# Sixteen batched products summed into one weight gradient: a new hand-written order, with A packed in three banks, set-aside places and GpSimd additions

## The chip, the cores and the metric

The kernel runs on one core of a Trainium2 chip. A core has a matrix engine (TensorE, "PE" in the profile, with its weight loads listed apart as "PEld"), a vector engine (DVE), a scalar engine (ACT), GpSimd (POOL) and a queue engine (SP). They work in parallel, each through its own instructions in order, and wait for one another through semaphores. PE writes its results into PSUM, eight banks of 512 fp32 columns on 128 partitions; everything else lies in SBUF. Transfers to and from the chip's memory are DMAs, issued here by SP, ACT and POOL. The metric is the device time of one execution in microseconds, lower is better, as the median of several runs.

## The reference

```python
batch, m, k, n = 16, 512, 1024, 768
input: (batch, m, k) float32;  grad_output: (batch, m, n) float32

def reference(input, grad_output):
    return np.einsum('bmk,bmn->kn', input, grad_output)   # (1024, 768) float32
```

Seen as one product, it is X.T @ G with X of 8192 x 1024 and G of 8192 x 768. The sum runs over all 8192 rows.

## The kernel before

The 8192 rows are cut into 32 "pairs" of 256 rows. Row 2p and row 2p+1 of a pair lie on the same partition, so a pair is two slices of 128 rows. Inputs are turned into bf16 by the loading DMAs (lines 152 and 153, on POOL's queue); the very first slice is loaded as fp32 through SP and ACT and rounded on DVE and ACT (`round_by`).

The output of 1024 x 768 is cut into four quarters by halves of k and n: A (first half of k, left half of n), B (first, right), C (second, left), D (second, right). Each quarter has four blocks q = 0 to 3 of 128 x 384.

A pair is multiplied in one of two ways, by its letter in `LOADS` (line 12):

- "s", plain: each of its two slices adds one matmul to each of the 16 blocks, 32 matmuls of 384 columns;
- "P", Strassen (in Winograd's form): the pair is treated as a 2 x 2 block product, with its two slices as the inner halves. Seven products per q replace eight: A, B, C and four more called 1, 5, 6 and 7, so 28 matmuls. For that DVE forms sums of operands: `sum_x` (tokens x0 to x2; lines 183, 185, 187) and `sum_g` (g0 to g2; lines 193, 195, 197). Results go into tiles `xe` and `ge`, and partly back into the pair itself.

In the end the products are combined: 6 gets 1 added, 7 gets 6 added, 5 gives two differences, and each of the quarters gets one of the shared sums added (`SHARED`, line 253).

There are 32 blocks (8 kinds times 4 q) that grow over the whole run, and eight PSUM banks. So a block is accumulated in a bank for some matmuls, then closed, that is, brought to its fp32 place in SBUF (`acc` for A to D, `macc` for 1, 5, 6, 7), and taken up again later. There are two ways round:

- *fill, then close by copy*: ACT copies the block's partial sum from SBUF into a bank (`fill`, line 274), PE goes on adding to it, and ACT (token c, line 327) or DVE (token v, line 329) copies the bank back;
- *start fresh, then close by addition*: PE starts a bank from nothing, and DVE adds the bank to the SBUF place (token v, line 331).

The final closing of a block (lines 307 to 312) adds the shared sum on DVE, and for A to D stores the block at once with a DMA (line 320).

The order of all this is written out by hand in `PLAN` (lines 22 to 77) as tokens, carried out one after the other; each engine's instructions come in the order of the tokens. `A0@7.1` opens block A0 in bank 7 and does one matmul; `A1.2` does two more matmuls on an open block; `fC0@2` fills bank 2 with C0; `vC0` and `cC0` close on DVE and on ACT; `x0.6` forms the first x-sums of pair 6; `r0` is a rounding. The last fill, `fB3@2+7`, splits a block over two banks as 256 and 128 columns, so that the last closing and its store come in two pieces.

Quarter A's four blocks stay in banks 7, 3, 4 and 1 during most of the run in the plan's first line (`A0@7`, `A3@3`, `A1@4`, `A2@1`) and are closed once, near the end. The other 28 blocks share banks 0, 2, 5 and 6.

Pairs are kept in a pool of `PAIRS_HELD` = 14 places, the operand sums in one of `SUMS_HELD` = 10 (lines 81 and 82). A load into a place waits until all that reads its old content is done. Before the data arrive, four matmuls on constants (`WARMUP`, line 80, bf16 and fp32) keep PE busy.

Of the kernel before, what the change touches and what calls it, by code (L numbers as in the profile page):

```python
# [9 lines left out]
P = 128  # L10

LOADS = "ssssssPPPPPPPPPPPPPPPPPPPPPPPPPs"

PLAN = (
    "A0@7.1 A3@3.1 A1@4.1 C3@5.1 C2@0.1 C1@2.1 r0 cC3 C0@6.1 vC2 A2@1.1 cC1 D0@5.1 vC0 B0@0.1 cD0 D1@2.1 "
    "r1 r3 B3@6.1 r2 D3@5.2 vB0 r4 A1.1 A2.1 cD1 vB3 A3.1 B1@0.2 cD3 B2@2.2 vB1 D2@6.2 cB2 C0@5.1 C1@0.1 "
    "vD2 A0.1 fD0@2 A2.1 vC0 A3.1 fD1@6 A1.1 D0.2 vC1 C2@5.2 cD0 D1.2 vC2 C3@0.2 cD1 B0@2.2 vC3 B3@5.3 "
    "fB1@6 vB0 A0.2 fB2@0 vB3 B1.2 fC0@2 B2.2 cB1 C1@5.2 vB2 C0.2 fD2@6 A3.1 vC1 D3@0.2 cC0 D2.2 fC2@5 "
    "vD3 C3@2.1 A1.1 cD2 A2.1 vC3 C2.1 B0@0.1 D1@6.1 vC2 D0@2.1 vB0 fD2@5 A3.2 vD1 A1.2 fB0@0 D2.2 vD0 "
    "B1@6.2 cD2 B0.2 vB1 B2@2.2 cB0 B3@5.2 vB2 C0@6.2 fC1@0 A2.2 vB3 fC2@2 C1.2 vC0 C3@5.2 cC1 C2.2 vC3 "
    "fD0@6 A0.2 D1@0.4 vC2 D3@5.4 vD1 D0.4 vD3 C3@2.2 vD0 B3@5.2 C0@0.2 vC3 fC1@6 A3.2 vB3 fB2@2 A0.2 vC0 "
    "C1.2 fD2@5 B2.2 cC1 D2.2 vB2 C2@0.2 cD2 B0@6.2 vC2 fB1@2 A1.4 vB0 fC1@0 B1.4 C2@5.2 cB1 D2@6.2 vC2 "  # L30
    "C1.2 fD0@2 A2.4 vD2 fD3@5 vC1 fC3@6 D0.2 D3.2 vD0 C3.2 cD3 C0@0.2 vC3 B2@2.4 vC0 fB3@6 B0@5.4 vB2 "
    "fD1@0 B3.4 fC0@2 vB0 A3.1 g0.6 fB1@5 A3.3 vB3 A0.2 g1.6 A0.2 fC1@6 D1.1 g2.6 D1.3 A2.2 vD1 A1.3 x0.6 "
    "fC2@0 C0.3 C1.1 x1.6 C1.2 cC0 C2.1 x2.6 C2.2 cC1 C3@2.1 g0.7 C3.2 cC2 B1.3 fD0@6 vC3 D2@0.2 g1.7 cB1 "
    "D0.2 vD2 fD3@2 A2.1 A3.1 A0.1 g2.7 cD0 10@5.1 D3.2 c10 x0.7 11@0.2 cD3 12@6.2 v11 13@5.2 c12 50@2.1 "
    "x1.7 50.1 c13 51@0.2 x2.7 52@6.2 c50 g0.8 53@5.2 c51 70@2.2 v52 c53 A2.1 g1.8 A3.1 fB3@0 72@6.2 v70 "
    "73@5.2 c72 g2.8 B3.2 v73 63@2.2 cB3 B2@6.1 x0.8 B2.1 fC1@5 A1.2 v63 A0.2 71@0.1 x1.8 71.2 vB2 62@2.3 "
    "c71 x2.8 C1.2 c62 g0.9 60@6.3 cC1 61@2.1 g1.9 61.2 fB0@0 v60 10@5.2 c61 g2.9 B0.3 v10 fC3@6 C2@2.2 "
    "cB0 x0.9 C2.1 C3.3 fC0@5 vC2 A2.2 f52@0 C0.1 x1.9 cC3 C0.2 A3.1 x2.9 A3.1 cC0 12@2.1 g0.10 12.1 52.2 "
    "f63@5 v12 B1@6.3 c52 g1.10 63.2 f13@2 vB1 11@0.2 c63 A0.1 g2.10 13.2 v11 72@5.2 c13 x0.10 A1.2 f51@0 "
    "53@6.2 v72 A0.1 f70@2 A3.1 51.1 x1.10 f50@5 51.2 v53 70.3 c51 x2.10 50.2 f73@6 g0.11 50.1 B3@0.3 c70 "  # L40
    "v50 73.2 fB2@2 g1.11 73.1 vB3 A2.1 f10@5 B2.2 c73 g2.11 B2.1 10.1 x0.11 10.2 cB2 C1@0.3 c10 x1.11 "
    "62@6.2 f71@2 vC1 A3.1 A1.1 f61@5 A0.1 x2.11 71.2 f60@0 g0.12 71.1 61.3 v62 c71 60.1 g1.12 60.2 c61 "
    "B0@2.1 g2.12 fB1@6 B0.2 v60 11@5.2 vB0 B1.2 fC0@0 A2.1 x0.12 A2.1 cB1 A0.1 C0.3 fC2@2 v11 A3.1 fC3@6 "
    "A1.1 x1.12 C2.3 cC0 x2.12 13@5.2 f53@0 g0.13 13.1 C3.3 cC2 v13 53.2 f52@2 g1.13 53.1 vC3 12@5.3 c53 "
    "g2.13 52.3 f72@6 v12 63@0.2 x0.13 c52 63.1 72.3 f62@5 v63 A2.1 f51@2 A1.1 x1.13 62.2 c72 51.1 x2.13 "
    "51.2 f50@0 v62 73@6.3 c51 g0.14 50.3 f70@5 v73 A3.1 fB2@2 A0.1 70.1 g1.14 c50 70.2 g2.14 B3@6.3 c70 "
    "B2.1 x0.14 B2.2 10@5.3 vB3 cB2 C1@0.1 x1.14 C1.2 f60@6 v10 11@2.3 x2.14 60.2 f61@5 g0.15 60.1 A1.1 "
    "61.3 c60 vC1 A0.1 g1.15 71@6.3 c61 v11 B0@0.1 fB1@5 g2.15 B0.2 v71 A2.2 fC2@2 A3.1 x0.15 A3.1 f52@6 "
    "B1.3 vB0 C2.2 cB1 x1.15 C2.1 52.2 cC2 x2.15 52.1 C0@0.1 fC3@5 g0.16 C0.2 A1.1 c52 A0.1 vC0 C3.3 "
    "f12@2 g1.16 13@6.3 vC3 12.2 g2.16 f62@5 12.1 v13 53@0.3 c12 x0.16 62.3 f72@6 A1.1 v53 63@2.3 c62 "  # L50
    "x1.16 f50@0 72.4 v63 f51@5 50.1 g0.17 50.2 c72 70@2.1 x2.16 70.2 c50 g1.17 51.3 v70 73@6.2 g2.17 c51 "
    "73.1 B2@0.1 x0.17 fB3@2 B2.2 A2.2 fC1@5 v73 B3.3 x1.17 C1.3 vB2 cB3 10@6.2 x2.17 cC1 10.1 71@0.1 "
    "g0.18 f11@2 71.2 A3.2 v10 f60@5 11.1 g1.18 11.2 v71 60.3 c11 g2.18 61@6.3 c60 x0.18 A0.3 fC0@2 v61 "
    "B1@0.3 fB0@5 x1.18 C0.3 fC2@6 vB1 B0.2 cC0 x2.18 B0.1 C2.1 g0.19 f12@0 C2.2 C3@2.3 cB0 vC2 12.2 "
    "f62@5 g1.19 12.1 vC3 A1.2 c12 53@6.1 g2.19 53.2 f52@2 x0.19 13@0.4 v53 A3.2 52.1 x1.19 f72@6 52.3 "
    "v13 62.2 x2.19 c52 62.2 g0.20 73@0.3 c62 g1.20 63@2.4 f51@5 v73 72.1 g2.20 72.2 fC1@0 v63 51.3 c72 "
    "x0.20 A2.3 c51 70@2.1 x1.20 70.3 f71@5 x2.20 50@6.4 v70 C1.1 g0.21 C1.2 fB2@2 A0.2 v50 cC1 B2.2 "
    "g1.21 B2.2 fB3@6 g2.21 A1.2 cB2 B3.4 x0.21 71.3 cB3 B0@0.2 x1.21 c71 B0.1 10@6.2 x2.21 10.2 vB0 "
    "C2@2.2 g0.22 C2.1 f61@0 A3.2 vC2 11@5.3 g1.22 11.1 f60@2 61.4 v10 g2.22 60.4 v11 c61 x0.22 C0@6.4 "
    "f53@0 c60 12@5.1 x1.22 12.3 vC0 B1@2.2 x2.22 B1.2 g0.23 C3@6.4 v12 53.2 g1.23 53.2 vB1 A1.2 c53 vC3 "  # L60
    "52@5.3 f73@2 g2.23 13@0.2 x0.23 13.2 A2.3 v52 A0.1 x1.23 A0.2 f51@5 v13 A3.2 51.1 x2.23 51.2 g0.24 "
    "51.1 73.3 c51 g1.24 73.1 C1@6.1 g2.24 C1.2 c73 63@5.4 vC1 f72@2 70@0.1 x0.24 f71@6 70.2 72.5 v63 v70 "
    "f62@5 A1.2 x1.24 c72 71.2 g0.25 71.2 f50@0 62.1 x2.24 fB2@2 62.2 g1.25 62.2 c71 B2.1 g2.25 B2.3 c62 "
    "50.4 vB2 B0@6.1 x0.25 f10@2 B0.3 c50 C2@5.1 x1.25 C2.3 f11@0 vB0 10.2 x2.25 10.2 g0.26 11.4 c10 vC2 "
    "B3@6.2 f60@2 g1.26 B3.2 c11 g2.26 B3.1 60.4 vB3 fB1@0 61@5.2 fC0@6 x0.26 61.2 c60 B1.4 v61 12@2.1 "
    "x1.26 fC3@5 12.3 vB1 C0.2 g0.27 f53@0 C0.2 x2.26 C3.2 cC0 g1.27 C3.2 v12 53.3 cC3 g2.27 53.1 52@6.4 "
    "v53 A2.1 x0.27 f51@0 A2.3 v52 A3.3 x1.27 A3.1 f70@6 A0.2 x2.27 A0.2 g0.28 A1.3 13@2.1 g1.28 13.2 "
    "g2.28 13.1 C1@5.4 v13 51.4 f73@2 vC1 70.1 x0.28 f63@5 70.3 c51 73.1 x1.28 73.3 c70 x2.28 73.1 63.2 "
    "c73 g0.29 63.3 f72@2 50@0.1 g1.29 50.2 c63 g2.29 50.1 71@6.4 v50 f62@5 72.4 fB0@0 v71 62.1 x0.29 "
    "f11@6 62.3 c72 B0.1 x1.29 B0.3 c62 x2.29 11.4 fB2@2 vB0 fC2@5 B2.1 g0.30 B2.4 f10@0 v11 C2.4 vB2 "  # L70
    "f11@6 10.1 g1.30 f12@2 10.3 vC2 A2.1 g2.30 A2.2 c10 x0.30 12.4 f13@5 f10@0 x1.30 11.1 13.3 c12 v11 "
    "10.1 A3.1 f61@2 x2.30 A3.2 v13 f62@6 A1.3 v10 f63@5 61.5 f60@0 62.2 v61 60.5 v62 f71@2 A2.2 f72@6 "
    "v60 A3.2 A1.2 vA2 f70@0 A0.5 vA3 vA1 70.3 vA0 63.2 v70 f50@1 71.2 72.2 fC0@3 v63 50.2 f73@0 v71 C0.6 "
    "f51@4 v72 fC1@5 v50 51.3 f52@2 fC2@7 C1.5 vC0 fD0@6 v51 fB0@1 52.4 fD1@3 B0.4 vC1 fB1@4 C2.3 v52 "
    "fD2@5 B1.7 vB0 fB2@2 vC2 73.2 vB1 B2.3 v73 f53@1 D0.2 D1.2 fC3@4 vB2 53.4 vD0 C3.6 vD1 v53 fD3@0 "
    "fB3@2+7 D2.2 D3.2 vC3 B3.7 vD2 vD3 vB3 "
).split()


WARMUP = [("b", 512), ("f", 512), ("f", 512), ("b", 512)]  # L80
PAIRS_HELD = 14
SUMS_HELD = 10

MERGED = 2


@with_exitstack
def kernel(
# [6 lines left out]
    nc = tc.nc  # L95
    bf16 = mybir.dt.bfloat16
    f32 = mybir.dt.float32
# [153 lines left out]


    SHARED = {"A": "1", "B": "5", "C": "7", "D": "1", "6": "1", "7": "6"}

    done = {(p, q): 0 for p in streams for q in range(Q)}
    fresh = {(p, q): True for p in streams for q in range(Q)}
    closed = set()
    opened = {}
    used = {7}
# [5 lines left out]
    def fill(p, q, b, b2):  # L265
        assert (p, q) not in opened and not fresh[p, q] and b in used
        src = sum_of(p, q)
        if b2 is None:
            parts = [(bank(b), 0, NH)]
        else:  # L270
            assert b2 in used
            parts = [(bank(b), 0, 256), (bank(b2), 256, NH)]
        for tile_, c0, c1 in parts:
            nc.scalar.copy(out=tile_[:, 0 : c1 - c0], in_=src[:, c0:c1])  # L274
        opened[p, q] = (parts, True)

    def multiply(p, q, b, n):
        first = (p, q) not in opened
        if first:
            opened[p, q] = ([(bank(b), 0, NH)], False)  # L280
            used.add(b)
        parts, carried = opened[p, q]
        for tile_, c0, c1 in parts:
            for j in range(n):
                at = done[p, q] + j
                stat, mov = operands(p, streams[p][at], q)
                nc.tensor.matmul(  # L287
                    tile_[:, 0 : c1 - c0],
                    stat,
# [7 lines left out]
    def close(engine, p, q):  # L297
# [34 lines left out]
        if final:  # L332
            closed.add((p, q))
# [51 lines left out]
```

## Time and profile before

| | |
|---|---|
| median of three runs | 162.09 us (162.0 to 162.27) |
| the profiled execution | 162.31 us |
| its span in the profile | 160.5 us |
| granted TensorE clock | 1.00 |
| instructions | 2776 |
| matmuls in the main loop (line 287) | 931 |
| ACT copies, fills (line 274) and closings (line 327) | 141 and 106 |
| DVE closing additions (line 331) and copies (line 329) | 95 and 38 |
| DMA busy until about 140 us | 99% |

The span is what the engines' records cover; the profiled execution took 1.8 us more than that. A group of the profile gives a source line, an engine, an operation, what is written and read, and the count; then the busy time and the mean duration of one. A duration runs from the start of an instruction until its last result is written, and the next instruction of the same engine may start before that, so the pace of an engine is read from start to start. Views used below are the busy times, the chain of work that ended last, the waits, and the timeline, in which rows give start (us), length (us), engine, line, operation and count.

### The profile page before, as it was taken

The page shows a single profiled execution, that of the slowest core. Times are in us where ns is not written, and L with a number is a line of the kernel's source. Part 1 is how long each engine was busy: PE and PEld are TensorE (multiplying, and loading weights), DVE is VectorE, ACT ScalarE, POOL GpSimd, SP SyncE. Part 2 cuts the span into 40 slices and gives each one's busy share as a digit, 9 for nine tenths or more (in the row PEclk, how much of TensorE's full clock was granted, in tenths as well). Part 3 has the DMA queues.
Part 4 walks back from the last instruction along what each step waited for, and adds up shares of the span by engine and source line. Part 5 has one row for each costly group of instructions (what it writes and reads, how often), then busy time and mean ns, then how long its engine had stood idle before and what let it go on. Part 6 is the DMA issues. An engine that isn't in the chain of part 4 may idle for free.

```text
span 160.5 us, 2776 instructions
## 1 busy us (share of the span) xinstructions
PE 155.3 (97%) x937; PEld 91.9 (57%) x937; DVE 142.7 (89%) x323; ACT 112.8 (70%) x253; POOL 34.8 (22%) x69
## 2 busy tenths in 40 slices
PE   8899999999999999999999999999999999999990
PEld 3355556556556656655655655665665665556560
DVE  0788986989999999999989998998899998989992
ACT  3779737749888999968777786534777368877730
POOL 7452222122221222222122222212222100000000
PEclk9999999999999999999999999999999999999999
DMA  5999999999999999999999999999999999924385
GB/s 176 295 213 213 210 216 213 213 213 212 213 212 212 213 213 214 210 214 213 215 214 213 213 212 212 213 212 214 213 210 213 215 212 214 212 43 157 137 294 196
DMA packets 12830, 33.40 MB, mean 208 GB/s; under 512 B 1424, under 2 KB 4624, under 8 KB 12816
## 3 DMA queue, kind: packets, MB, share of 16 engines
q0 software_dynamic: 9360, 28.64, 90.2%
q1 hardware_dynamic: 3024, 3.47, 6.3%
q10 hardware_dynamic: 432, 1.11, 1.8%
q8 instruction: 7, 0.11, 0.3%
q14 instruction: 7, 0.06, 0.1%
HBM read 58.72 MB, written 3.15 MB: 385 GB/s over the span
## 4 chain that ended last, share of the span: by engine, by line
DMA 48%; PE 44%; DVE 2%; issue 2%; POOL 1%; DVEq 0%; POOLq 0%
DMA xp<-in_input_dram 48%; PE bank L287 44%; POOL gp L157 1%; DVE acc L312 1%; DVE xe L183 0%; POOL xp L159 0%; DVE acc L331 0%; DVE macc L331 0%; DVEq L380 0%; DVE xe L185 0%; POOLq L153 0%; POOLq L369 0%; POOLq L152 0%
## 5 line engine op out<-in xcount | busy, mean ns | idle before, releaser
L287 PE MATMUL bank<-gp,xp 128*128 128x384 bf16 (+2 forms) x631 | 109.8, 324 | 0.6 <-DVE xp L201 0.6
L287 PEld LDWEIGHTS <-xp 128*128 128x128 bf16 x631 | 61.1, 98 | 42.5 <-DVE xp L201 1.3
L287 PE MATMUL bank<-ge,xe 128*128 128x384 bf16 x300 | 56.2, 326 | 0.1
L274 ACT COPY bank<-macc 128x384 f32<-128x384 f32 x71 | 33.6, 484 | 13.2 <-DVE macc L331 5.6
L287 PEld LDWEIGHTS <-xe 128*128 128x128 bf16 x300 | 29.3, 98 | 19.9 <-issue 0.6
L274 ACT COPY bank<-acc 128x384 f32<-128x384 f32 (+1 forms) x70 | 32.3, 479 | 9.1 <-DVE acc L329 5.5
L327 ACT COPY macc<-bank 128x384 f32<-128x384 f32 x61 | 28.6, 479 | 9.5 <-PE bank L287 8.1
L331 DVE TENSOR_TENSOR acc<-bank,acc 128x384 f32<-128x384 f32 x54 | 28.7, 552 | 2.8 <-PE bank L287 1.2
L153 POOL DMA_DIRECT2D xp<-in_input_dram x30 | 16.0, 532 | 53.3 <-DMA xp<-in_input_dram 28.0
L327 ACT COPY acc<-bank 128x384 f32<-128x384 f32 x45 | 21.4, 480 | 6.5 <-PE bank L287 6.0
L152 POOL DMA_DIRECT2D gp<-in_grad_output_dram x30 | 16.0, 533 | 37.1 <-DMA gp<-in_grad_output_dram 15.0
L331 DVE TENSOR_TENSOR macc<-bank,macc 128x384 f32<-128x384 f32 x41 | 22.5, 551 | 0.5 <-PE bank L287 0.2
L183 DVE TENSOR_TENSOR xe<-xp 128x1024 bf16<-128x1024 bf16 x25 | 17.1, 683 | 1.2 <-DMA xp<-in_input_dram 1.2
L329 DVE COPY acc<-bank 128x384 f32<-128x384 f32 x24 | 13.1, 553 | 3.0 <-PE bank L287 2.4
L193 DVE TENSOR_TENSOR ge<-gp 128x768 bf16<-128x768 bf16 x25 | 13.8, 550 | 0.0
L187 DVE TENSOR_TENSOR xp<-xp,xe 128x512 bf16<-128x512 bf16 x25 | 10.5, 419 | 0.4
L185 DVE TENSOR_TENSOR xe<-xe,xp 128x512 bf16<-128x512 bf16 x25 | 10.5, 418 | 0.3
L197 DVE TENSOR_TENSOR gp<-ge,gp 128x384 bf16<-128x384 bf16 x25 | 8.8, 352 | 0.3
L195 DVE TENSOR_TENSOR ge<-gp,ge 128x384 bf16<-128x384 bf16 x25 | 8.7, 350 | 0.2
L312 DVE TENSOR_TENSOR acc<-bank,macc 128x384 f32<-128x384 f32 (+2 forms) x17 | 8.0, 522 | 0.0
L329 DVE COPY macc<-bank 128x384 f32<-128x384 f32 x14 | 7.6, 552 | 0.4 <-PE bank L287 0.4
L201 DVE CAST gp<-gf 128x192 bf16<-128x192 f32 (+1 forms) x2 | 0.7, 360 | 4.9 <-DMA gf<-in_grad_output_dram 4.9
(17 smaller groups left out, 21.6 us busy)
## 6 DMA issues: line engine op xcount, KB each, us to landing
xp<-in_input_dram POOLq DMA_DIRECT2D x30, 512.0 KB, 16.9
gp<-in_grad_output_dram POOLq DMA_DIRECT2D x30, 384.0 KB, 16.7
out_dram<-acc SPq DMA_DIRECT2D x12, 192.0 KB, 1.9
xf<-in_input_dram ACTq DMA_DIRECT2D x2, 512.0 KB, 5.0
gp<-in_grad_output_dram POOLq DMA_DIRECT2D x3, 192.0 KB, 6.6
out_dram<-acc SPq DMA_DIRECT2D x6, 96.0 KB, 1.7
xp<-in_input_dram POOLq DMA_DIRECT2D x2, 256.0 KB, 8.0
gf<-in_grad_output_dram SPq DMA_DIRECT2D x2, 192.0 KB, 4.2
```

The lines of the kernel that those rows point to most:

```text
L152: nc.gpsimd.dma_start(out=gp, in_=G[rows, :].rearrange("(p m) n -> p m n", m=2))
L153: nc.gpsimd.dma_start(out=xp, in_=X[rows, :].rearrange("(p m) k -> p m k", m=2))
L183: nc.vector.tensor_sub(out=xe[:, 0:2, :], in0=x[:, 1::-1, :], in1=x[:, 3::-2, :])
L185: nc.vector.tensor_sub(out=xe[:, 2, :], in0=xe[:, 0, :], in1=x[:, 0, :])
L187: nc.vector.tensor_add(out=x[:, 1, :], in0=x[:, 2, :], in1=xe[:, 2, :])
L193: nc.vector.tensor_add(out=ge[:, 0:2, :], in0=g[:, 0:2, :], in1=g[:, 1::2, :])
L274: nc.scalar.copy(out=tile_[:, 0 : c1 - c0], in_=src[:, c0:c1])
L287: nc.tensor.matmul(tile_[:, 0 : c1 - c0], stat, mov[:, c0:c1], start=first and j == 0, stop=True, skip_group_check=True,)
L312: nc.vector.tensor_add(out=dst[:, c0:c1], in0=b, in1=sum_of(SHARED[p], q)[:, c0:c1])
L327: nc.scalar.copy(out=dst, in_=b)
L329: nc.vector.tensor_copy(out=dst, in_=b)
L331: nc.vector.tensor_add(out=dst, in0=b, in1=dst)
```

## The change

- `LOADS`: four plain pairs at the start instead of six; one at the end as before.
- Quarter A's blocks are opened with `@R` (resident) and packed into three banks, 5, 6 and 7 (`resident_parts`): A0 in bank 5; A1 as 128 columns in bank 5 and 256 in bank 6; A2 as 256 columns in bank 6 and 128 in bank 7; A3 in bank 7. Each step on A1 or A2 is two matmuls. Only the first matmul into each of these banks carries the start flag. The other blocks have banks 0 to 4.
- A block may be closed by an ACT copy even when its bank was started from nothing: the copy goes to one of 16 set-aside places in SBUF (`aside`), and a later fill with the suffix `s` brings it back into a bank instead of the block's sum. Seven closings are of this kind.
- New tokens p and q: an addition of the shared sum on GpSimd (`add_shared`). `p62` adds it to a block's SBUF sum before the last closing, which is then a plain DVE addition; `qA1` does it after an ACT closing and then stores the block. There are nine.
- `SHARED` for D is 6 instead of 1, and 5's second difference is left in block 6's place.
- `PLAN` is a new order throughout. `PAIRS_HELD` is 11 instead of 14, `SUMS_HELD` 8 instead of 10. `WARMUP` is one bf16 matmul of 512 columns and 32 of 128.

```diff
-LOADS = "ssssssPPPPPPPPPPPPPPPPPPPPPPPPPs"
+LOADS = "ssssPPPPPPPPPPPPPPPPPPPPPPPPPPPs"
 PLAN = (
-    "A0@7.1 A3@3.1 A1@4.1 C3@5.1 C2@0.1 C1@2.1 r0 cC3 C0@6.1 vC2 A2@1.1 cC1 D0@5.1 vC0 B0@0.1 cD0 D1@2.1 "
+    "A0@R.1 C0@0.1 C3@1.1 cC0 r0 cC3 C1@0.1 C2@2.1 A1@R.1 vC1 A2@R.1 cC2 A3@R.1 B1@3.1 r1 r3 D0@4.1 r2 B0@1.1 "
...
+    "12.1 f71@3 12.1 g2.30 61.2 x2.30 c12 61.2 v63 f73@1 71.1 p62 71.1 v61 71.1 f53@2 71.1 73.1 62@4.1 fD3@0 "
+    "62.1 v73 p60 53.3 v71 A1.3 v62 D3.2 cA1 v53 A3.1 p72 A3.2 f52@4 A3.1 A0.2 cA3 52.1 vD3 pC3 72@1.2 A2.1 "
+    "vA0 A2.1 fB2@0 A2.2 v72 fD2@5 A2.1 qA1 C3@3.2 v52 f70@1 C3.2 60@2.1 cA2 60.1 pC1 B2.2 v60 f51@6 B2.2 D2.1 "
+    "vC3 fB1@4 D2.1 pC2 70.1 51.1 fD1@7 vD2 51.2 f50@3 B1.1 vB2 B1.1 qA3 B1.2 v51 fD0@0 B1.2 C1@2.2 qA2 C1.1 "
+    "v70 C1.1 50.2 vC1 50.2 C2@6.1 vB1 C2.1 fB0@1+2 C2.2 v50 D0.1 fB3@5 D0.1 D1.2 fC0@4 B3.2 vD1 B3.3 vC2 B3.1 "
+    "C0.2 vD0 C0.3 vB3 B0.2 vC0 B0.5 vB0 "
...
-WARMUP = [("b", 512), ("f", 512), ("f", 512), ("b", 512)]
-PAIRS_HELD = 14
-SUMS_HELD = 10
+WARMUP = [("b", 512)] + 32 * [("b", 128)]
+PAIRS_HELD = 11
+SUMS_HELD = 8
...
-    SHARED = {"A": "1", "B": "5", "C": "7", "D": "1", "6": "1", "7": "6"}
+    SHARED = {"A": "1", "B": "5", "C": "7", "D": "6", "6": "1", "7": "6"}
...
+    def resident_parts(q):
...
+        a, b, c = (resident[i] for i in (5, 6, 7))
+        return [
+            [(a, 0, 0, NH)],
+            [(a, NH, 0, 128), (b, 0, 128, NH)],
+            [(b, 256, 0, 256), (c, 0, 256, NH)],
+            [(c, 128, 0, NH)],
+        ][q]
...
+    def fill(p, q, banks, from_aside):
...
+        if from_aside:
+            slot = asides[p, q].pop(0)
+            free_asides.append(slot)
+            src = aside[:, slot, :]
...
+                fresh = first and j == 0
+                if fresh and where == "R":
+                    fresh = tile_.name not in begun
+                    begun.add(tile_.name)
...
+    def close(engine, p, q, queue):
...
+        away = engine == "c" and not carried
+        if away:
+            asides[p, q].append(free_asides.pop(0))
+            dst = aside[:, asides[p, q][-1], :]
...
+    def add_shared(p, q, prepare, queue):
+        assert (SHARED[p], q) in closed
+        dst = sum_of(p, q)
+        nc.gpsimd.tensor_add(out=dst, in0=dst, in1=sum_of(SHARED[p], q))
+        if prepare:
...
+            prepared.add((p, q))
+        else:
...
+            closed.add((p, q))
+            store(p, q, 0, NH, queue)
```

As built, SP's queue does not take the output stores in the plan's order: the store of A1 (after `qA1`) stands first, then those of D3, A0, A3 (after `qA3`), A2 (after `qA2`), C3, D2, B2, C1, B1, D1, C2, D0, B3, C0 and B0's first part; B0's second part is on ACT's queue. POOL's queue has, between its last load and its first addition, an instruction that reloads GpSimd's code.

## The prediction

> **What bounds the kernel now.** I read the page first (busy times, chain that ended last), then the waits of PE and PEld, then short stretches of the timeline for the pace of each engine.
>
> ```profile
> span 160.5 us, 2776 instructions
> PE 155.3 (97%) x937; PEld 91.9 (57%) x937; DVE 142.7 (89%) x323; ACT 112.8 (70%) x253; POOL 34.8 (22%) x69
> ```
>
> PE is nearly always busy. The chain, back from the end, is matmuls to 84 us, and before that loads:
>
> ```profile
> 64.61 17.76 DMA xp<-in_input_dram
> ...
> 84.41 70.98 PE bank L287 x435
> 155.39 0.36 DVE acc L312
> ```
>
> 435 matmuls in 70.98 us are 163 ns each. The loads before them bound little: PEld waited 1.0 us for them in all.
>
> ```profile
> PEld L287 <- DVE xp L201: 1.3, 1, 1.3
> PEld L287 <- DMA xp<-in_input_dram: 1.0, 4, 0.4
> PEld L287 <- ACT xp L201: 0.5, 2, 0.3
> ```
>
> The pace of each width is read off the weight loads near the end (each matmul has one): ten in a row at 384 columns, seven at 256, then 128.
>
> ```profile
> 153.75 1.56 PEld L287 LDWEIGHTS <-xp 128*128 128x128 bf16 x10
> 155.54 0.75 PEld L287 LDWEIGHTS <-xp 128*128 128x128 bf16 x7
> 156.31 0.38 PEld L287 LDWEIGHTS <-xp 128*128 128x128 bf16 x6
> ```
>
> A load lasts 98 ns, so start to start is (1.56-0.098)/9 = 162.5 ns, (0.75-0.098)/6 = 109 ns and (0.38-0.098)/5 = 56 ns. The kernel has 7 plain pairs of 32 matmuls and 25 Strassen pairs of 28: 924 of full width, seven of them split, 924 x 0.1625 = 150.2 us. First matmul at 5.19, last at 156.6: PE lost some 1.3 us between. **PE sets the time**; ahead of it lie 5.2 us of first loads, behind it the last additions and a store (issued at 157.42, 2.1 us to landing: 159.5), then 1 us. The profiled run took 162.31: 160.5 of span and 1.8 around it. The median is 162.09, 0.22 less, so I take differences from the profiled run to the median.
>
> **The change, part by part.**
> *Two pairs fewer plain:* 5 x 32 + 27 x 28 = 916 matmuls, -8 x 0.1625 = **-1.30 us** of PE. DVE gains two pairs of sums, 2 x 2.77 by the page's means, and loses nine closing additions (9 x 0.55) against four more mid-run (4 x 0.55): +2.8 us of its 142.7. It stays under PE.
>
> *A in three banks:* A1 and A2 are cut into 128 and 256 columns, 37 matmuls each: 74 splits, each 109 + 56 - 162.5 = 2.5 ns, **+0.18 us**. Bounds: nothing, and 98 ns each (every weight load exposed), 7.3 us; the rows above show 128-column matmuls with a load each at 56 ns, so I take 2.5.
> The Trainium skill, "TensorE: Matmul & The Clock Gate", section "Back-to-back issue gap", speaks against the change: it gives about 81 ns a matmul for sustained load-and-matmul pairs at 128 columns. By it the splits would cost 74 x 0.028 = 2.0 us (an estimate from that page); the trace's 56 ns disagrees, though over seven matmuls only.
>
> *Five working banks instead of four, and the new order.* Banks 0 to 4 are free for the other blocks. ACT pays: by the plan, 160 fills and 136 closings (140 and 106 before, and 5 roundings in each), and 224 ACT instructions stand within the first 90 us of matmuls. ACT's own pace:
>
> ```profile
> 51.82 0.48 ACT L327 COPY macc<-bank 128x384 f32<-128x384 f32 x1 [0.33 <-PE bank L287]
> 52.19 1.31 ACT L274 COPY bank<-macc 128x384 f32<-128x384 f32 x3
> ```
>
> A closing holds ACT 0.37 (51.82 to 52.19), a fill (1.31-0.48)/2 = 0.415. 113 fills, 106 closings and 5 roundings (0.3 each) are 87.6 us, **97% of 90**; before, the same stretch held 162:
>
> ```profile
> 8.00:98.00 90.00, 89.81 (x551) 53.51 (x550) 84.03 (x189) 71.23 (x162) 23.24 (x44) 1.00 1.07 213
> ```
>
> (PE, PEld, DVE, ACT, POOL.) PE's work hides this only while ACT never falls 2 to 4 us behind. I take PE's mid-run idle as unchanged, 0.9 us; bounds -0.6 (five banks remove most of it) and +2 (below). The seven set-aside closings are ACT copies, counted in the 136. That `5` leaves its second difference in block 6's place instead of block 1's moves no work, and with 8 sum tiles a pair's sums are last read before the pair eight later is summed: nothing for either.
>
> *The head.* The fourth matmul now reuses bank 0. C0 waits for its rounding (the three DVE roundings end at 5.40), its result comes 0.33 later, cC0 takes 0.48, so C1 starts at about 6.35; until 8.0 that makes 13 matmuls where PEld counts 15 before: **+0.35 us**. The warm-up runs before the data: 0.38 us for the first 512 columns (0.78 to 1.16), a quarter of it for each of 32: 4.2 us, under 5.19. If no weight load overlapped (0.10 more each) it ended at 7.4: +2.2 us.
>
> *Loads.* Each issue waits for the load four pairs earlier, and pairs land every 4.35 us (17.40 us for four in the chain), so the issue of u falls on the landing of u-4. By the plan the pair 11 before is last read some 15 us earlier than that: the smaller pool costs nothing. The first Strassen pair is first read 20.35 us of matmuls in, 5.19 + 20.35 + 0.5 = 26.0, and lands near 25.4 (29.7 - 4.35): 0.6 us of cover.
>
> *GpSimd.* POOL is idle after its last load:
>
> ```profile
> 125.62 0.53 POOL L153 DMA_DIRECT2D xp<-in_input_dram x1 [1.89 <-DVE macc L329]
> ```
>
> Then come a reload of its code and nine additions. The first (p62) can start when c12 is out: 134.9 us of matmuls in, 141.5, plus 0.16 + 0.48: 142.2. So the reload has 16 us; bounds 0 and, by the longest row, the 16.9 us that a queued load takes to land: hidden or up to 1 us late. One addition d: no row; below, DVE's 0.55 of the same shape; above, 1.28, the longest single instruction off PE (ACT's table load). I take the middle, 0.9.
> The skill's "GPSIMD Engine Reference", section 3.1, measures about 2.6 cycles an element at 1.2 GHz: an estimate of 0.83 us here, and section 2.1 some 6 us for the first call of newly loaded code. No run here shows either; by them both hide.
> Behind an addition wait DVE closings (v62, v72, v60, vC3, vC1, vC2), and **SP's queue**: the built order puts the store of A1 before D3's and A0's, and those of A3 and A2 before C3, D2, B2, C1 and all that follow. v62 is out at about 144.7 (137.3 + 6.7 + 0.2 + 0.5) and seven additions follow: A2 at 144.7 + 7d = 151.0. It lands 1.9 later, and eleven stores of 192 KB behind it need 0.54 each (363 GB/s at 157 to 158.5): 151.0 + 1.9 + 5.9 = 158.8. By PE the last store lands at 159.5 - 0.77 = 158.75. They tie: SP hides at 0.9, and from there each 0.1 us of d costs 0.7.
>
> **Sum:** -1.30 + 0.18 + 0.35 = -0.77 us; profiled 162.31 - 0.77 = 161.5, median **161.3**.
>
> **Rivals.**
> (1) *GpSimd's stores hold SP* (slower). At d = 1.2 the end is 144.7 + 8.4 + 7.8 = 160.9, +1.4: 163.5. It decides from d = 1.0 on. For: the queue order; against: only the estimate of d. 0.13.
> (2) *ACT becomes the bound* (slower). The waits of before hold single ACT waits of 2.5 us and more:
>
> ```profile
> ACT macc L327 <- PE bank L287: 8.1, 12, 2.5
> ACT bank L274 <- DVE acc L329: 7.7, 9, 2.7
> ```
>
> Two of these (5.2) in the first 90 us outrun its slack (91 - 87.6 = 3.4) by 1.8: 163.1. Against: with 38% of its time free ACT had no reason to hurry there. 0.10.
> (3) *The splits cost 81 ns*, +1.8: 163.1. The row speaks against. 0.04.
> (4) *The gain doesn't show:* d near 1.0, 0.7 us more ACT waits, or loads (0.6 us of cover) hold PE: 162.1. 0.13.
> (5) The forecast, faster by 0.4 to 1.7: 0.60.
>
> **How the numbers follow.** Faster 0.60, slower 0.13 + 0.10 + 0.04 = 0.27, same 0.13; 0.2% (0.32 us) is about what this kernel's measurement can tell (its runs span 0.27). The forecast's own range is 160.4 (mid-run idle gone, -0.6, and 0.3 of tail) to 161.8. To hold 8 in 10 it must take in the unchanged case and part of (1) to (3): 160.4 to 163.3.
>
> **What would show it.** Right: PE starts 997 matmuls of the main loop, the last near 155.9; PE idle near 1.6 us; POOL additions of 0.8 to 1.0 us, the first before 143; ACT over 95% busy from 8 to 98. Wrong: PE idle waiting for banks that ACT holds; SP waiting for POOL past 151.5; a first matmul after 5.3; 128-column matmuls over 60 ns apart.

## The result, and the profile after

The changed kernel took 163.26 us, median of 5 runs (162.74 to 163.47), against 162.10 before: a ratio of 1.0053 (95% interval 1.0040 to 1.0066). Twelve more runs later gave 162.93 (162.59 to 163.72), ratio 1.0040 (1.0024 to 1.0056). It is slower by some 0.4 to 0.5%, where 0.77 us faster was forecast. The profiled run took 163.41, with a span of 161.6. Some runs of kernels with this head and warm-up, though none of these 17, are 1.4 to 2.5 us longer; the last section shows what they have.

The page's first lines, span and busy time of each engine:

```profile
span 161.6 us, 3045 instructions
PE 154.7 (96%) x1030; PEld 97.5 (60%) x1030; DVE 144.7 (90%) x330; ACT 125.5 (78%) x302; POOL 43.4 (27%) x78
```

PE is busy 0.6 us less and the span is 1.1 us longer. The chain of work that ended last (start, length, engine, line) still runs through the matmuls, now for 813 of them instead of 435, and ends on VectorE's additions:

```profile
26.00 123.45 PE bank L335 x813
...
155.03 1.80 DVE acc L375 x4
156.84 0.20 DVEq L448
```

It stops at 157.04, and the span at 161.6: what the chain doesn't show is the 4.6 us in which only stores and the program's end are left. The same step, from the timeline of VectorE before and after (start, length; five additions each):

```profile
155.39 2.00 DVE L312 TENSOR_TENSOR acc<-bank,macc 128x384 f32<-128x384 f32 x5
```

```profile
155.03 2.00 DVE L375 TENSOR_TENSOR acc<-bank,macc 128x384 f32<-128x384 f32 x5
```

VectorE ends at 157.03 instead of 157.39: **the computation did become 0.36 us shorter**. The last store lands at 160.73 instead of 159.57, by the trace's transfer records. So from VectorE's end to the last landing it is 3.69 us instead of 2.18, and these 1.51 us less 0.36 are the 1.15 us lost. The question is what fills the 1.5 us.

The view of the output tensor gives the store issues on SP's queue and on ACT's (shortest, median, longest issue in ns, first and last start in us), and below them the time from an issue to its landing, that is, until the data are written:

```profile
L295 SPq DMA_DIRECT2D out_dram<-acc x19: 348/406/1762, 148.1 to 158.2; - x19
L295 ACTq DMA_DIRECT2D out_dram<-acc x1: 372/372/372, 157.1 to 157.1; - x1
...
DMA to landing us min/median/max: 1.7/2.2/3.4
```

The first store is issued at 148.1 (before: 144.35), one issue takes 1762 ns where the median is 406, and the last is issued 1.2 us after VectorE has finished. SP's own waits name what the first store waited for (total, times, longest; SP had nothing to issue after the loads at the start, so this one wait is long):

```profile
SPq L295 <- POOL acc L392: 146.5, 1, 146.5
```

Line 392 is GpSimd's addition; it is A1's, which stands first in SP's queue. The microseconds 149 to 153 by the windows view (window; its length; busy time of PE, PEld, DVE, ACT, POOL, each with its instructions; PE clock; DMA share; GB/s):

```profile
149.00:150.00 1.00, 1.00 (x8) 0.61 (x7) 1.00 (x3) 1.00 (x4) 1.00 (x3) 1.00 0.56 179
150.00:151.00 1.00, 1.00 (x8) 0.61 (x7) 1.00 (x3) 0.66 (x2) 1.00 (x3) 1.00 0.05 7
151.00:152.00 1.00, 1.00 (x8) 0.59 (x6) 0.97 (x3) 0.20 (x1) 0.93 (x1) 1.00 0.56 181
152.00:153.00 1.00, 1.00 (x8) 0.59 (x6) 1.00 (x3) 0.68 (x3) 0.00 (x0) 1.00 0.66 208
```

The last column is the point: with stores waiting in the queue, 7 GB/s in the whole microsecond from 150 to 151. The traffic from 147.9 to 151 has a second customer beside the stores, which are on q1 (packets, MB, share):

```profile
q1 hardware_dynamic: 280, 0.19, 20.1%
q8 instruction: 1, 0.02, 2.9%
```

That is one 16-KB transfer of instructions; by its record it begins at 148.94 and takes 1434 ns, where the seven before it took 893 to 974. The long issue begins at 148.99.

### The profile page after: what moved, and what is told of

It reads as the page before. It is cut to its first block, busy times and chain, and to the rows that moved or that the text cites. A ratio compares the mean times of both kernels' runs of the same rounds, so it can differ in the third digit from the quotient of the medians.

```text
span 161.6 us, 3045 instructions
## 1 busy us (share of the span) xinstructions
PE 154.7 (96%) x1030; PEld 97.5 (60%) x1030; DVE 144.7 (90%) x330; ACT 125.5 (78%) x302; POOL 43.4 (27%) x78
## 4 chain that ended last, share of the span: by engine, by line
PE 89%; DVE 4%; DMA 3%; issue 1%; ACT 0%; DVEq 0%
PE bank L335 89%; DMA xf<-in_input_dram 3%; DVE acc L375 2%; DVE macc L370 1%; DVE macc L368 1%; DVE acc L382 0%; ACT acc L360 0%; DVE xp L206 0%; DVEq L448 0%; DVE macc L375 0%; DVEq L375 0%
## 5 line engine op out<-in xcount | busy, mean ns | idle before, releaser
L335 PEld LDWEIGHTS <-xp 128*128 128x128 bf16 x673 | 63.1, 98 | 38.3 <-DVE xp L206 1.3
L335 PE MATMUL bank<-ge,xe 128*128 128x384 bf16 x324 | 65.0, 326 | 0.0
L313 ACT COPY bank<-macc 128x384 f32<-128x384 f32 x86 | 40.7, 493 | 7.2 <-DVE acc L382 4.6
L360 ACT COPY macc<-bank 128x384 f32<-128x384 f32 x77 | 36.0, 505 | 10.7 <-PE bank L335 10.5
L335 PEld LDWEIGHTS <-xe 128*128 128x128 bf16 x324 | 31.4, 98 | 19.6
L382 DVE TENSOR_TENSOR macc<-bank,macc 128x384 f32<-128x384 f32 x47 | 25.6, 551 | 1.3 <-PE bank L335 1.1
L360 ACT COPY acc<-bank 128x384 f32<-128x384 f32 (+2 forms) x52 | 23.8, 476 | 3.1 <-PE bank L335 2.7
L380 DVE COPY acc<-bank 128x384 f32<-128x384 f32 x22 | 11.6, 552 | 2.5 <-PE bank L335 1.7
L392 POOL TENSOR_TENSOR macc<-macc 128x384 f32<-128x384 f32 x3 | 3.0, 997 | 16.7 <-ACT macc L360 16.2
L392 POOL TENSOR_TENSOR acc<-acc,macc 128x384 f32<-128x384 f32 x6 | 5.8, 1003 | 0.0
```

Of the source, the lines that this page charges most:

```text
L313: nc.scalar.copy(out=tile_[:, at : at + c1 - c0], in_=src[:, c0:c1])
L335: nc.tensor.matmul(tile_[:, at : at + c1 - c0], stat, mov[:, c0:c1], start=fresh, stop=True, skip_group_check=True,)
L360: nc.scalar.copy(out=to, in_=b)
L380: nc.vector.tensor_copy(out=to, in_=b)
L382: nc.vector.tensor_add(out=to, in0=b, in1=to)
```

## The experiments

Theory when they began: the prediction's first rival, that GpSimd's additions hold SP's stores. Main competitors: the loss is in the matmuls (ACT's banks, the splits, the head), or the transfers as such limit the tail. Each kernel was timed in five rounds beside the kernel before, some twelve runs of it unless a smaller number is given. The column "tail" is the time from the end of VectorE's last addition to the last landing, in the profiled run; it leaves out what the head did in that run.

| kernel | median us | ratio to before (95%) | DVE ends | last landing | tail |
|---|---|---|---|---|---|
| before | 162.1 to 162.5 | 1 | 157.39 | 159.57 | 2.18 |
| changed | 163.26 | 1.0053 (1.0040 to 1.0066) | 157.03 | 160.73 | 3.69 |
| changed, again | 162.93 | 1.0040 (1.0024 to 1.0056) | 157.02 | 160.99 | 3.98 |
| stores in finishing order | 161.94 | 0.9987 (0.9968 to 1.0006) | 156.65 | 159.23 | 2.58 |
| instruction transfer moved | 162.36 | 1.0016 (0.9994 to 1.0038) | 157.05 | 159.80 | 2.75 |
| the same, one addition more | 163.36 | 1.0102 (1.0064 to 1.0140) | 156.81 | 160.65 | 3.83 |
| order and head | 161.76 | 0.9964 (0.9950 to 0.9978) | 156.69 | 159.15 | 2.46 |
| order, head, transfer moved | 161.70 | 0.9958 (0.9944 to 0.9971) | 156.81 | 159.08 | 2.26 |

The interval of "the same, one addition more" is wide because two of its seven runs are the long kind; the other five lie at 163.31 to 163.45.

**1. SP's stores in the order in which blocks are finished.** SP was not among the engines that keep the plan's order:

```
-    ctx.enter_context(tc.manual_schedule(engines={E.PE, E.DVE, E.Activation, E.Pool}))
+    ctx.enter_context(tc.manual_schedule(engines={E.PE, E.DVE, E.Activation, E.Pool, E.SP}))
```

> The changed kernel with one difference: SP's stores stand in the order in which their blocks are finished (D3 and A0 first, then A1, C3, D2, B2, A3, A2, then the rest). Theory (GpSimd's stores hold SP): in the changed kernel the last additions of VectorE end at 157.0 us, 0.4 earlier than before, but the store queue ends at 160.7, since A2 lands at 154.75 and eleven stores of 0.54 us stand behind it. Here eight stand behind A2, so the queue would be done by 153.8 + 8 x 0.54 = 158.1, and the last store waits for its own block: issued near 157.1, landed near 159.2, span 160.2, about 161.9 us in all (1.4 below the changed kernel's 163.3, and level with or just below the 162.1 before). Rival (the loss is in the matmuls: ACT holds banks, or the splits): nothing changes, 163.2. Rival (the output transfers as such are the limit whatever their order): no more than 0.5 us gained, 162.8.

Measured 161.94, 1.0 to 1.3 below the changed kernel's two medians. PE's, VectorE's, ACT's and POOL's work is the same, so the loss is not in the matmuls. SP's waits now:

```profile
SPq L295 <- DVE acc L375: 145.2, 2, 144.9
...
SPq L295 <- POOL acc L392: 1.3, 1, 1.3
```

VectorE's D3 releases the first store at 146.5. The 1.3 us that the view puts down to GpSimd are no wait for an addition: they lie inside one issue, A1's, which begins at 148.38, after A1's addition has ended (147.70), and takes 1828 ns beside an instruction transfer (148.46 to 149.84). So the pause is still there, and no store waits for GpSimd any more; A2's goes out at 152.74, 1.2 after its addition. B0's first part, issued last, goes out at 156.70, 0.05 after its addition.

**2. Whole stores.** The first three stores are not cut (rows of 1536 bytes instead of 768): `HALVED = 0`.

> The changed kernel with one difference: no store is cut in two, where the first three stores were cut into halves of 192 columns (rows of 768 bytes). SP's order is that of the changed kernel. Theory (GpSimd's additions alone hold SP): A2 is added at 151.9 whatever the first stores do, lands near 153.8 instead of 154.75, and the eleven stores behind it end near 159.8: 162.3 us, 1.0 below the changed kernel. If only the queue order matters and the halves do not, 163.2; if the slow halves at the queue's head (206 GB/s against 363) are the whole loss, 162.0 or less.

Measured 162.44 (three of the twelve runs are of the long kind): 0.5 to 0.8 gained, where the theory had 1.0. **3. Both:**

> Both differences together: SP's stores in the order in which blocks are finished, and none cut in two. Theory (the tail is held by the store queue alone): once the queue's order is mended the last store waits for its block, so whole stores add nothing: 161.9 us, as with the order alone. Rival (halves and order are two separate costs): they add up, 161.2 or less. Rival (the loss is in the matmuls): 163.2.

Measured 162.15, with eight of its twelve runs at 161.89 to 162.51 and four of the long kind; no better than the order alone. The two edits don't add up: both let the same queue catch up.

**4. The head.** C1's first run takes the unused bank 3, and 0 and 3 are exchanged from there on:

```
- A0@R.1 C0@0.1 C3@1.1 cC0 r0 cC3 C1@0.1 C2@2.1 ... B1@3.1 r1 r3 D0@4.1 r2 B0@1.1 r4 B3@0.1
+ A0@R.1 C0@0.1 C3@1.1 cC0 r0 cC3 C1@3.1 C2@2.1 ... B1@0.1 r1 r3 D0@4.1 r2 B0@1.1 r4 B3@3.1
```

> The changed kernel with one difference: the first run of block C1 goes to bank 3, which is still unused, instead of bank 0, which waits for C0's closing; from there on banks 0 and 3 are exchanged throughout. The first matmuls lost 0.85 us in the changed kernel's profile, 0.57 of it just before C1. Theory: 0.3 to 0.5 us less PE idle at the head, and as the additions of GpSimd start from a finished matmul, the whole tail moves with it: 162.8 to 163.0 us. Rival (the head's loss is taken up by a later wait, for loads or for ACT): 163.2.

Measured 162.90, ratio 1.0032 (1.0018 to 1.0046): 0.1 to 0.3 us by the two ratios of the changed kernel, not clear by itself. **5. With the order** it is:

> SP's stores in the order in which blocks are finished, and C1's first run in bank 3: the two edits that each helped alone. Theory (the order moves the tail back onto VectorE's last additions, and the head then moves these): 161.94 less the head's 0.36 = 161.6 us in the undisturbed runs. In one profile (whole stores) the matmul clock fell to 0.50 from 6.6 to 10.2 us, after PE had been idle from 4.3 to 5.3 and again before C1, and the run was 1.8 us longer; if the idle time ahead of C1 is part of the cause, fewer such runs here than the 8 of 36 in the three first experiments, if the time between the warm-up's end and the first matmul is enough, as many. Rival (the head's gain is taken up in the tail): 161.9.

Measured 161.76 in ten runs, ratio 0.9964 against 0.9987: 0.37 us from the head, and the first of the kernels that is faster than before by more than the interval. The wait shows in PE's timeline, the changed kernel first, then this one:

```profile
5.43 0.94 PE L335 MATMUL bank<-gp,xp 128*128 128x384 bf16 x3 [0.65 <-DVE xp L206]
6.78 21.17 PE L335 MATMUL bank<-gp,xp 128*128 128x384 bf16 x141 [0.40 <-ACT acc L360]
```

```profile
5.26 22.34 PE L335 MATMUL bank<-gp,xp 128*128 128x384 bf16 x144 [0.48 <-DVE xp L206]
```

The 0.40 us for which PE waited for cC0 (line 360) are gone, and 144 matmuls run without a break that the view separates. This profile can't show the whole gain: its first matmuls start 320 ns apart instead of 162.5, since the clock comes up only at 6.61 (last section).

**6. With the warm-up of the kernel before:**

> As the run before, with the warm-up of the kernel before (512 bfloat16 columns, twice 512 float32 columns, 512 bfloat16 columns), which ended at 4.63 us there, where the 33 short ones ended between 4.27 and 4.78. Theory (the late clock falls where PE idles too long after the warm-up): no run 1.8 us above the others, as in 35 of 35 runs of the kernel before, and the undisturbed runs as in the run before: 161.6. Rival (the long runs come from something else, the loads or the host): they stay.

No long run in twelve, but 162.34, 0.6 slower than the run before: a miss. VectorE ends at 156.67, as in that run (156.69), yet the last SP store is issued at 157.31 instead of 156.73. The store issues say why:

```profile
L295 SPq DMA_DIRECT2D out_dram<-acc x19: 332/383/979, 146.5 to 157.3; - x19
```

One takes 979 ns; it begins at 154.77, beside an instruction transfer at 154.44. With 29 warm-up matmuls fewer the transfer had moved from 148.7 to 154.4, where the queue had no time left to catch up. This made the pause a suspect of its own.

**7 and 8. One GpSimd addition more**, ahead of A2's, in the changed kernel and in the one with SP in order:

```
+        if (p, q) == ("A", 2):
+            nc.gpsimd.tensor_add(out=spare, in0=dst, in1=sum_of(SHARED[p], q))
         nc.gpsimd.tensor_add(out=dst, in0=dst, in1=sum_of(SHARED[p], q))
```

> The changed kernel with one GpSimd addition more: the last of the nine (A2's) is done twice, the first time into a spare place that nobody reads. Theory (GpSimd's stores hold SP, and eleven stores of 0.54 us behind A2's end the run): the whole 0.96 us of the addition comes out at the end, 164.2 us. Rival (the tail is bound by the transfers or by the matmuls): 163.3.

> The same spare addition, with SP's stores in the order in which blocks are finished. Theory: A2 is out at 152.9 instead of 151.9; eight stores of 0.49 us of issue follow it, so that B0's first part is issued at 152.95 + 8 x 0.49 = 156.9, 0.2 later than without: 161.9 to 162.2 us, against 161.94. Rival (GpSimd's additions themselves hold VectorE or PE in the tail): the 0.96 us shows here as well, 162.9.

Measured 163.40 (six runs) and 161.94. The second was as expected; **the first went against the theory**: by the ratios (1.0058 against 1.0053 and 1.0040) the addition cost 0.1 to 0.3 us. In the changed kernel A2's addition ends at 151.93, but SP reaches its store at 152.77 only: 0.84 us of cover, made by the long issue. The first kernel has no profile to compare: the run that was profiled took 183.45 us at a granted clock of 0.85.

**9. The transfer moved by another warm-up**, 57 matmuls for the same columns, and **10.** the same in kernel 5:

```
-WARMUP = [("b", 512)] + 32 * [("b", 128)]
+WARMUP = [("b", 512)] + 8 * [("b", 128)] + 48 * [("b", 64)]
```

> The changed kernel with another warm-up: 48 of 64 columns for 24 of the 32 of 128 columns, the same number of columns in 24 more matmuls. In every profile so far a 16-KB instruction transfer lies beside a stretch of 0.6 to 1.4 us in which one store's issue on SP takes that much longer (1.76 instead of 0.4 us in the changed kernel, beside a transfer that begins at 148.94 and takes 1.43 us instead of 0.9), and its place moves with TensorE's number of instructions: 29 warm-up matmuls fewer moved it from 148.7 to 154.4 us. Theory (the late start of the store queue and this collision add up): 24 matmuls more move it to about 144, ahead of the first store; the queue then starts at 148.1 without a pause, A2 goes out at 152.0, and eleven stores of 0.54 us after 153.85 end at 159.8 instead of 160.7: 162.3 us. Rival (the transfer has nothing to do with the pause, SP's queue pauses by itself after its first few stores): 163.2.

> The same warm-up in the fastest kernel so far (stores in the order in which blocks are finished, C1's first run in bank 3). Theory: there the queue has already caught up when B0 is done (issued 0.03 us after its addition), so moving the pause gives at most what the transfers in flight still hold, 0 to 0.3 us: 161.5 to 161.75 against 161.76. Rival (the longer row of short warm-up matmuls ends later, holds the first matmul or drops the clock): 162 or more, or some runs 1.8 us longer.

Measured 163.18 (seven runs) and 162.36: both miss, by 0.9 and 0.6. In the first one's profile no issue pauses and the tail is 2.75 us, as the theory has it, but its head ran at half the clock, so that VectorE ended at 158.72. The transfer had moved by some 2 us, not 5, and in the second it met the first stores (148.08 against 148.11). The second one's profile is of a long run too (163.25). What this warm-up costs at the head in ordinary runs no profile caught; it stays open.

**11. The additional addition ahead of A1's**, the first store, in the changed kernel (same edit, `("A", 1)`):

> The changed kernel with the spare GpSimd addition ahead of A1's instead of A2's. A2's second addition changed little (163.4 against 163.3), since SP came to A2's store only at 152.77, 0.8 us after it was ready. Theory (it is the first store that is held: A1's, at 148.05, with all the others behind it in a queue that never catches up): SP starts 0.96 us later and the end comes 0.7 to 1.0 us later, 164.0 to 164.3. Rival (the pause beside the instruction transfer alone sets the queue's end, whatever the first store waits for): no more than 0.3 us, 163.6 or less.

Measured 163.32 (three of eleven runs are of the long kind, the profiled one among them): the rival's side. The long issue ends 0.36 us after the instruction transfer here (152.20 and 151.84) and 0.38 in both profiles of the changed kernel, whatever SP waited for before.

**12. The changed kernel again** (third row of the table), on the same chip as the next three:

> The changed kernel unchanged, beside the others of this call, so that all four share one chip and the same runs of the kernel before. 163.1 to 163.3 us, and, if its runs too can fall into the 1.8 us longer kind that the first experiments showed, one to three of twelve near 165.

Measured 162.93, 0.2 below what was expected, and no long run.

**13. The transfer moved without touching head or queue.** A0's matmuls are cut in two, 37 TensorE matmuls and their weight loads more:

```
         parts, carried = opened[p, q][-1]
+        if p == "A" and q in (0,):
+            ((tile_, at, _, _),) = parts
+            parts = [(tile_, at, 0, 256), (tile_, at + 256, 256, NH)]
```

> The changed kernel with A0's 37 matmuls cut into 256 and 128 columns: 37 matmuls and 74 TensorE instructions more, at 2.5 ns each, 0.1 us, and a head and a warm-up that stay as they were. The instruction transfer beside the stores moves from 148.9 to between 143 and 146, ahead of the first store at 148.1. Theory (a store queue that starts late, and is paused once by that transfer): no store's issue takes over 0.5 us, A2's store follows its addition at 152.0, eleven of 0.54 after its landing near 153.85 end at 159.8 instead of 160.7; 0.8 us less than the changed kernel, 162.4. Rival (the pause is SP's own): 163.3.

Measured 162.36 (162.21 to 162.49 but for two long runs), 0.6 below the changed kernel of experiment 12, where 0.8 was expected. Its store issues, and the windows of the changed kernel's pause:

```profile
L295 SPq DMA_DIRECT2D out_dram<-acc x19: 332/402/441, 148.1 to 157.3; - x19
```

```profile
149.00:150.00 1.00, 1.00 (x8) 0.61 (x7) 1.00 (x3) 1.00 (x4) 1.00 (x3) 1.00 0.63 202
150.00:151.00 1.00, 1.00 (x8) 0.61 (x7) 1.00 (x3) 0.66 (x2) 1.00 (x3) 1.00 0.65 208
151.00:152.00 1.00, 1.00 (x8) 0.60 (x7) 0.97 (x3) 0.21 (x1) 0.95 (x1) 1.00 0.66 212
```

No issue is longer than 441 ns, and 208 GB/s move where 7 did. The transfer begins at 144.62, before the first store, and takes 919 ns. SP is idle before A2's store, issued at 151.97 right after the addition; it lands at 153.84, and eleven times 0.54 later, at 159.80, the last one: to 0.02 us what the expectation worked out.

**14 and 15. The same cut in kernel 5, and in kernel 6** (there A0 and A3):

> The same cut of A0 in the fastest kernel so far. The queue has caught up there by the end, so the pause costs nothing: 161.76 + 0.1 for the cuts = 161.85 us, or 161.6 if the last store's landing (2.43 us after its issue, 2.15 in the kernel before) gains from a queue that is less full. Rival to the reading of the other warm-up's loss (0.6 us in both kernels that had it): were the moved transfer its cause and not the warm-up, this one would be near 162.4 as well.

> The fastest kernel so far with the warm-up of the kernel before, and A0 and A3 cut in two, which brings the instruction transfer from 154.4 us back to 144 to 149. Theory (with that warm-up alone the transfer met the store queue at 154.4, too late to catch up, and cost 0.5 us): 161.8 us, and no long runs. Rival (the old warm-up itself costs 0.5 us): 162.3.

Measured 161.70 (five runs) and 162.02 (eight). The first is the fastest kernel of the study, 0.6 us below before and 1.2 below the changed one; from kernel 5's 161.76 it can't be told apart. The second, 0.2 above its expectation, has no pause and a tail of 2.28 instead of experiment 6's 2.83; in its profile PE waited 0.18 and 0.31 us for loads, at 9.8 and 22.1 us, that most others had in time. So the tail gives back nearly all of the 0.58 us that the old warm-up lost, the medians 0.32: the pause was more than half of that loss, and whether the old warm-up itself has a part in the rest stays open. By elimination, the loss of experiments 9 and 10 is that of their warm-up.

**16. The additional addition, without the pause:**

> The kernel with the transfer moved ahead of the stores (162.36), with the spare GpSimd addition ahead of A2's. In the changed kernel this addition did nothing, since the pause had already put SP 0.8 us behind it; here SP waits for A2 (its store is issued at 151.97, straight after the addition, with SP idle before it). Theory (A2's store with eleven behind it sets the end once the pause is gone): all 0.96 us come out at the end, 163.3 us. Rival (the end hangs on the pause alone, or on VectorE): 162.4.

Measured 163.36, 1.00 us more than without it (on another chip, where the kernel before took 162.25 instead of 162.31). SP's waits, first without, then with the addition (total, times, longest):

```profile
SPq L295 <- POOL acc L395: 147.0, 2, 146.5
```

```profile
SPq L295 <- POOL acc L398: 147.9, 2, 146.3
```

Apart from the first wait, for A1, SP waits 0.5 us and then 1.6 us for GpSimd; A2's store goes out at 152.81. **With the pause out of the way the whole addition on GpSimd comes out at the end.**

## Why the prediction was wrong

The forecast fell on one step, "They tie: SP hides at 0.9". The first rival, "GpSimd's stores hold SP", was the case, at 0.13, and the end that its terms give, with the durations measured, is that of experiment 13. That its 163.5 lies so near the 163.26 measured is luck: it took an addition of 1.2 us, and knew nothing of the pause, which makes up the difference.

*What it computed with.* The prediction had A2 out at 144.7 + 7d = 151.0 with d = 0.9. GpSimd's timeline (start, length, count):

```profile
142.76 1.96 POOL L392 TENSOR_TENSOR macc<-macc 128x384 f32<-128x384 f32 x2 [16.25 <-ACT macc L360]
145.17 1.00 POOL L392 TENSOR_TENSOR macc<-macc 128x384 f32<-128x384 f32 x1 [0.45 <-DVE macc L382]
146.13 5.80 POOL L392 TENSOR_TENSOR acc<-acc,macc 128x384 f32<-128x384 f32 x6
```

An addition takes 1.00 us, and six in a row (5.80 - 1.00)/5 = 0.96 from start to start. The third starts at 145.17, 0.5 later than the 144.7 taken. So A2 was out at 151.93, 0.93 late: half of it the start, half of it seven times 0.06. (The prediction's mark "SP waiting for POOL past 151.5" shows in experiment 13, at 151.96; in the changed kernel the pause covers it.) The Trainium skill's "GPSIMD Engine Reference", section 3.1, from which the prediction estimated 0.83, is further off than the 0.9: the trace has 1.00. The rest of the sum, 1.9 to land and 0.54 for each of eleven stores, was right in experiment 13 (153.84 - 151.97 = 1.87; 159.80). There the queue alone turns the forecast gain into 1.0016, no change. A tie was taken as hidden, although the prediction itself had put the point of decision a tenth of a microsecond away.

*What it left out.* In the changed kernel the end is another 0.93 us later (160.73 against 159.80): the pause beside the instruction transfer. The prediction counted stores and their transfer time and had no term for it, though the trace of before has such a transfer, its seventh, at 144.14, with one issue of 0.73 us beside it, where the queue had 13 us to recover. With the change TensorE has 192 instructions more as built; the seventh transfer begins at 132.51 and an eighth at 148.94, and the queue's start is put at 148.1. Experiment 13 shows the pause to follow the transfer; how the one stops the other no run shows.

*The halves* of the first stores (0.4 us more each by their landings, 206 GB/s instead of 363) were counted only as part of the queue's order; in a queue that runs without slack they cost 0.5 to 0.8 (experiment 2).

*The computation*, -0.77 forecast, -0.36 by VectorE's end:
- Eight matmuls fewer at 162.5 ns: right. 
- The splits at 2.5 ns: right. 37 more of them in experiment 13 move VectorE's end by 0.02 to 0.04 us (157.05 against 157.03 and 157.02); the third rival's 28 ns each, which comes from the Trainium skill's 81 ns ("TensorE: Matmul & The Clock Gate", section "Back-to-back issue gap"), would be 1.0. The trace disagrees with that figure for these short runs of 128 columns.
- The head, 0.35: PE waited 0.40 at C1 as worked out, which kernel 5 gave back (0.37). But the first matmul started at 5.43, above the 5.3 that the prediction had set as a mark; in the other undisturbed profiles with this warm-up it started between 5.21 and 5.37. It follows the loads, and before's 5.19 is one draw of it: some 0.1 to 0.2 of the shortfall.
- PE's idle time between first and last matmul, from start to start, came to 1.96 us, 1.6 forecast; the rest of the shortfall is single waits of 0.03 to 0.19 us for banks between 17 and 37 us, 0.8 us in all, each of them ended by an ACT copy. The 0.9 us of mid-run idle, taken as unchanged, became 1.1.
- Second rival, ACT becomes the bound: no. It is as full as worked out (88.49 of 90 us, 98%; 97% forecast), but PE loses those short waits to it, not the rival's 1.8 us (whose slack was taken from 91 us, elsewhere from 90). The busy time, 89.97 of 90, doesn't show them, because a matmul of 384 columns lasts 326 ns and the next starts after 162.5: a wait of less than the difference leaves no gap:

```profile
8.00:98.00 90.00, 89.97 (x593) 55.80 (x592) 86.35 (x196) 88.49 (x220) 22.93 (x44) 1.00 1.07 213
```

- GpSimd's code load hides (16.2 us of waiting ahead of the first addition), and so do the loads: the last lands at 142.76, before at 142.71.

So of the 1.5 us by which the tail grew, 0.9 is the pause (by experiment 13's profile), and 0.6 the late A2 with eleven stores behind it. Either cure, order or a moved transfer, takes most of it, because each gives the queue the time that the other cause uses up.

## What to carry to other kernels

A queue of stores has a start, a length and an end: when a change moves the store that stands first, or one with many behind it, work out the end from there (issue + landing + count times transfer time), and where it ties with the engine that computes, take the tie as a loss. Look at which engines a hand-written order binds: SP was left out, and a single word (`E.SP`) was worth 0.5% (0.9987 against 1.0040 at the least). An experiment that shows no effect may be covered by another stall: the addition that cost 0.1 to 0.3 us in the changed kernel cost its full 1.0 us once the pause was gone.

## What the hardware showed

**An instruction transfer stops stores.** In 12 of the 13 profiles in which a 16-KB transfer met stores in SP's queue, one issue took 0.73 to 2.08 us instead of 0.4, and the transfer up to 1.71 us instead of 0.9 (in experiment 16, ahead of the stores, 1.20); in the changed kernel 7 GB/s were stored in a whole microsecond of it. In the one left (experiment 3) the issue took 0.58, and a landing 3.7 us. In all 13 that issue ended 0.36 to 0.39 us after the transfer, however long the transfer took; in the five profiles whose transfer ended before the first store no issue took over 0.54. The transfers lie 16 to 22 us apart, and their place moves with the number of TensorE's instructions: 54 fewer in the warm-up moved the first from 17.1 to 21.2 us. The pause's length varies (1.76 and 2.08 us in two profiles of the changed kernel), and so do that kernel's runs, 162.59 to 163.72; with the transfer moved (experiment 13) they lie within 0.3 us, but for two long ones.

**The clock can fall after the warm-up, or come up late.** This is experiment 2's profiled run, one of the long ones (164.26):

```profile
5.00:6.00 1.00, 0.52 (x3) 0.22 (x4) 0.82 (x4) 0.71 (x2) 0.64 (x2) 1.00 1.06 371
6.00:7.00 1.00, 0.60 (x4) 0.28 (x3) 0.24 (x1) 0.81 (x2) 0.00 (x0) 0.96 1.13 232
7.00:8.00 1.00, 1.00 (x7) 0.67 (x5) 0.92 (x3) 0.66 (x3) 0.00 (x0) 0.50 1.16 208
8.00:9.00 1.00, 1.00 (x4) 0.46 (x3) 0.04 (x1) 0.49 (x3) 0.61 (x2) 0.50 1.13 213
9.00:10.00 1.00, 1.00 (x4) 0.46 (x3) 0.69 (x2) 0.84 (x2) 0.45 (x1) 0.50 1.15 207
```

The third column from the end is the granted clock. By its records it is 0.50 from 6.92 to 10.34 us, some 3.4 us, which costs half of that, 1.7 us. The Trainium skill's "TensorE: Matmul & The Clock Gate", section "Part 1: The HAM clock gate (the "warmup" mystery)", has a free-running window of about 3.4 us at whose end the clock is set by how busy TensorE was; the length agrees. In the 3.41 us before the fall PE was busy for 1.79 us, 52%; in experiment 9's profile, where the clock falls too, it was 55%, and in experiment 3's, where it stays up, 60%. PE had run its warm-up from 0.78 to 4.27 and then stood still for 1.07 us, and again ahead of C1.

The long runs profiled in experiments 10 and 11 (163.25 and 165.34) have another course. Here are experiment 10's weight loads, one for each matmul:

```profile
8.99 0.15 PEld L335 LDWEIGHTS <-xp 128*128 128x128 bf16 x1 [0.17 <-issue]
9.31 0.15 PEld L335 LDWEIGHTS <-xp 128*128 128x128 bf16 x1 [0.17 <-issue]
9.63 0.10 PEld L335 LDWEIGHTS <-xp 128*128 128x128 bf16 x1 [0.17 <-issue]
```

From start to start it is 320 ns, half the pace, from 6.1 until 9.6, and the first record of the clock lies there (9.62; 9.52 in experiment 11). So the clock had not come up before; the windows view shows 1.00 ahead of the first record, and is not to be trusted there. In the other profiles the first record lies between 3.5 and 6.6 us.

With C1's wait mended no run of 27 with the same warm-up was long, against 18 of 100 without (the 183.45 of experiment 7 not counted), and with the warm-up of the kernel before none of 20. That the idle time at the head is the cause is likely by this; the two kernels with 57 warm-up matmuls had long runs with and without the mended head, and no run tried the gap alone.
